# A two-layer diffusion trunk: part of attention's vector work moved to GpSimd, and the order around it

## The chip, the cores and the metric

The kernel runs on one core of a Trainium2 chip. The metric is the device time of one execution in microseconds (us); the kernel before took 3193.55 us (median of three runs, 3193.33 to 3194.81). The engines are TensorE (PE in the profile; PEld is its weight load), VectorE (DVE), ScalarE (ACT), GpSimd (POOL) and SyncE (SP), which issues the DMAs. Each takes its instructions in the order of the program, and waits at an instruction whose operands are not ready.

## The reference

Two layers over 1152 tokens: 128 prompt tokens and 1024 sample tokens, which share the weights. A layer projects the normalised tokens, runs three head groups (latent attention, a short convolution, retention), then an output projection and a SwiGLU mixer, all in float32. The change touches attention alone. For each of 8 heads:

```
q = rmsnorm(rmsnorm(q_lat) @ w_q_up, q_head_g)              # 96 per head: 64 plain + 32 rotary
k, v = ckv @ w_kv_up ; k = rmsnorm(concat(k_nope, k_pe), k_head_g)
sample: q, k rotated on the 32 columns; keys = 1024 sample + 128 cached context tokens
prompt: keys = its own 128 tokens, not rotated
p = softmax(q k^T * 96**-0.5) ; out = p @ v
```

## The kernel before

Heads are worked in four pairs. `pair_prep` (L930) makes q, k and v of a pair: for ten tiles of 128 tokens, nine or three matmuls, copies by ScalarE, and sums of squares (L978, L980). Then come the steps that this text calls the pair's chain: the mean squares (L983 to L986), an inverse square root in 11 small instructions (`rsq`, L231), the rotary steps (`rope`, L911: two products of 128x256 and two sums of 128x128 for each of two halves), and the products of q and k with the inverse norms (L994 to L997). `prompt` (L1008) scales the prompt's own q and k (L1015 to L1018), transposes them on TensorE (L1021) and does the prompt's whole attention in three steps. All these elementwise steps are VectorE's.

`head_prep` (L1056) transposes a head's k and q (L1069), splits them into a high and a low part (L1072 on ScalarE, L1073 on VectorE), and finds the maximum of each query's scores: 24 matmuls (L1080), each followed by a VectorE reduction (L1082); the maxima are negated (L1087), transposed (L1089) and written as eight more rows of q (L1091). `head_main` (L1097) then goes over nine key tiles: six matmuls for the scores (L1126 to L1128), two exponentials on ScalarE (L1129), and, one tile later in `pv`, the product with v (L1109) and the sum of the exponentials of all key tiles into `acc`, eight additions of 128x1024 on GpSimd (L1112, L1118); the last is halved between GpSimd and VectorE (L1116). `head_end` (L1145) multiplies `acc` with ones (L1152), takes the reciprocal by Ln, Exp and one Newton step (L1156 to L1159) and scales the output (L1161). It is issued within the next head, by `finish` after that head's first scores (L1131).

The parts are generators. `attention` (L1167) advances a head's nine tiles step by step (18 steps) and lets the next head's preparation and the next pair's preparation run a set number of steps beside it (`RA`, `RB`); a pair is `ready` `GAP` = 5 steps after its chain, and its prompt part follows. The instructions so issued are then placed by a scheduler that works with estimated durations, so each engine's order can differ from the order of the code. The first pair of a layer is prepared within the input projection (`in_proj`, L811), beside matmuls of L227 to L229 and the convolution (L829 to L838); pairs 2 to 4 within heads 1 to 4 of `attention`. PSUM has three buffers for scores (`mm`) and five for everything else (`ax`); the exponentials, `acc`, the query tiles and raw weights share twelve buffers `W`.

Of the kernel before, what the change touches and what calls it, by code (L numbers as in the profile page):

```python
# [39 lines left out]
EPS = 1e-6  # L40
SCALE = 96.0 ** -0.5
# [35 lines left out]
class Net:  # L77
# [165 lines left out]

# [666 lines left out]

    def rope(self, x, tab, out=None):  # L911

        nc = self.nc
# [3 lines left out]
        nc.vector.tensor_tensor(t1, x, tab[:, 0].unsqueeze(2).to_broadcast(sh), op=ALU.mult)  # L917
        nc.vector.tensor_tensor(t2, x, tab[:, 1].unsqueeze(2).to_broadcast(sh), op=ALU.mult)
        nc.vector.tensor_tensor(out[:, :, :, 0:16], t1[:, :, :, 0:16], t2[:, :, :, 16:32], op=ALU.subtract)
        nc.vector.tensor_tensor(out[:, :, :, 16:32], t2[:, :, :, 0:16], t1[:, :, :, 16:32], op=ALU.add)  # L920

# [8 lines left out]
    def pair_prep(self, l, p, R):  # L930

        nc = self.nc
        wh, wl = self.pair_weights(l, p, R)
        qh, ql = R["qn"]
# [18 lines left out]
        for t in range(10):  # L953
# [28 lines left out]
        V = nc.vector  # L982
        V.tensor_tensor(ssq[:, 2:4, :], ssq[:, 2:4, :], R["kvs2"].unsqueeze(1).to_broadcast([P, 2, 10]), op=ALU.mult)  # L983
        V.tensor_tensor(ssq[:, 2:4, :], ssq[:, 2:4, :], R["kpss"].unsqueeze(1).to_broadcast([P, 2, 10]), op=ALU.add)
        V.tensor_scalar(ssq[:, 2:4, :], ssq[:, 2:4, :], 1.0 / 96, EPS, ALU.mult, ALU.add)
        V.scalar_tensor_tensor(ssq[:, 0:2, 0:9], ssq[:, 0:2, 0:9], 1.0 / 96,  # L986
                               R["qms"].unsqueeze(1).to_broadcast([P, 2, 9]), ALU.mult, ALU.add)
# [20 lines left out]
    def prompt(self, l, p, R):  # L1008
# [3 lines left out]
        at = self.attn_tile(p, R)  # L1012
        gains = self.gains(l)
        for hh in range(2):
            V.tensor_tensor(pr[:, hh, 64:96], pr[:, hh, 64:96], R["gq"], op=ALU.mult)  # L1015
            V.tensor_scalar(pr[:, hh, :], pr[:, hh, :], r[:, hh, 0:1], None, ALU.mult)
            V.tensor_scalar(pr[:, 2 + hh, 0:64], pr[:, 2 + hh, 0:64], r[:, 2 + hh, 0:1], None, ALU.mult)
            V.tensor_scalar(pr[:, 2 + hh, 64:96], R["kper"][:, 0, :], r[:, 2 + hh, 0:1], None, ALU.mult)  # L1018
        pt = self.ax((96, 4, P))
# [36 lines left out]
    def head_prep(self, l, h, R):  # L1056
# [20 lines left out]
        for qt in range(8):  # L1077
# [8 lines left out]
        nc.vector.reduce_max(mn, mx, axis=AX.X)  # L1086
        nc.vector.tensor_scalar(mn, mn, -1.0, None, ALU.mult)  # L1087
# [3 lines left out]
        nc.vector.tensor_tensor(  # L1091
            qh[96:104, :].rearrange("p (a b) -> p a b", b=P), pt.unsqueeze(1).to_broadcast([8, 8, P]),
            self.vec[0:8, o:o + 8].unsqueeze(2).to_broadcast([8, 8, P]), op=ALU.mult)
        R["T", h] = (qh, ql, kh, kl)
        yield CM

    def head_main(self, l, h, R):  # L1097
# [8 lines left out]
        def pv(kt):  # L1106
            for qc in range(2):
                qs = slice(qc * 512, (qc + 1) * 512)
                nc.tensor.matmul(po[64 * qc:64 * qc + 64, :], vv[:, kt, b:b + 64], prs[kt][:, qs],  # L1109
                                 start=(kt == 0), stop=(kt == 8))  # L1110
            if kt == 1:
                nc.gpsimd.tensor_tensor(acc, prs[0], prs[1], op=ALU.add)  # L1112
            elif kt == 8:
                for e, eng in enumerate((nc.gpsimd, nc.vector)):
                    s = slice(512 * e, 512 * e + 512)
                    eng.tensor_tensor(acc[:, s], acc[:, s], prs[kt][:, s], op=ALU.add)  # L1116
            elif kt > 1:
                nc.gpsimd.tensor_tensor(acc, acc, prs[kt], op=ALU.add)  # L1118
        for kt in range(9):
# [3 lines left out]
            for qc in range(2):  # L1123
# [21 lines left out]
    def head_end(self, h, R, po, acc):  # L1145
# [8 lines left out]

        y, t = self.Tt("dy", (P, 512)), self.Tt("dt", (P, 512))
# [11 lines left out]
    def attention(self, l, R, x):  # L1167
# [10 lines left out]
        def pairs():  # L1178
            for p in range(1, 4):
                yield from self.pair_prep(l, p, R)  # L1180
                if p < 3:
                    self.pair_weights(l, p + 1, R)
                for _ in range(GAP):
                    yield
                R["ready", p] = True
                yield
                yield from self.prompt(l, p, R)
            while self.head_lim < 7:
                yield
            yield from self.mix_load(mix, range(6), A)  # L1190
# [570 lines left out]
```

## Time and profile before

| | |
|---|---|
| runs | 3193.33, 3193.55, 3194.81 us |
| the profiled execution | 3189.09 us, span 3187.2 us, mean granted clock 0.975 |
| busy share of the span | PE 96%, PEld 84%, DVE 56%, POOL 37%, ACT 35% |
| the chain that ended last | PE 80%, DVE 13%, ACT 2%, DMA 2%, POOL 1% |
| attention of the two layers | about 368 to 705 us and 1940 to 2280 us |

A stretch's row gives each engine's busy time and the granted TensorE clock as a share of 2.4 GHz (0.5 is the level of 1.2 GHz). Idle time of PE and time at the lower clock are what a stretch can give back; a busy PE is not always at its peak.

### The profile page before, as it was taken

How to read it: one execution, taken by the hardware profiler on the slowest of the kernel's cores; microseconds unless marked ns; L12 is line 12 of the kernel's file. 1: busy time of each engine (PE TensorE's matmuls, PEld its weight loads, DVE VectorE, ACT ScalarE, POOL GpSimd, SP SyncE). 2: the span in 40 equal slices, each digit the busy share in tenths (PEclk: the TensorE clock that was granted, in tenths of full speed). 3: DMA queues.
4: the chain of work that ended last, by engine and by line, in shares of the span. 5: the costliest groups of instructions: out<-in, count | busy, mean ns of one | idle time of the engine just before them, and what ended most of it. 6: DMA issues, size and time to landing. Idle time of an engine off the chain costs nothing.

```text
span 3187.2 us, 48870 instructions
## 1 busy us (share of the span) xinstructions
PE 3045.1 (96%) x19136; PEld 2692.7 (84%) x19136; DVE 1794.0 (56%) x3555; ACT 1112.9 (35%) x2646; POOL 1179.8 (37%) x764
## 2 busy tenths in 40 slices
PE   6999998999799999999999999889998999999999
PEld 5878855459799999998999897554697999999999
DVE  6264466776855455643272655767578554546343
ACT  4323354353432222321153234554344222223211
POOL 3111244455643434311242113435656434343212
PEclk9999998999899999999999999989998999999999
DMA  5323100123221222476231110001322222226323
GB/s 210 115 71 102 54 12 5 53 84 120 71 82 64 82 83 74 171 257 231 74 113 48 31 49 12 12 11 50 108 100 79 83 80 68 66 78 218 99 68 100
DMA packets 126726, 278.07 MB, mean 87 GB/s; under 512 B 24096, under 2 KB 47392, under 8 KB 126496
## 3 DMA queue, kind: packets, MB, share of 16 engines
q1 hardware_dynamic: 126496, 274.95, 25.6%
q8 instruction: 151, 2.47, 0.3%
q14 instruction: 79, 0.65, 0.1%
HBM read 222.57 MB, written 52.33 MB: 86 GB/s over the span
## 4 chain that ended last, share of the span: by engine, by line
PE 80%; DVE 13%; ACT 2%; DMA 2%; issue 2%; POOL 1%; SPq 0%; DVEq 0%; POOLq 0%; ACTq 0%
PE mm L227 14%; PE mm L229 14%; PE mm L228 13%; PE ax L229 6%; PE ax L227 6%; PE ax L228 6%; PE ax L1109 5%; PE ax L1080 2%; PE mm L1126 2%; PE mm L1128 2%; PE mm L1127 2%; PE ax L340 1%; PE ax L1069 1%; DVE mx L1082 1%; POOL W L213 1%
## 5 line engine op out<-in xcount | busy, mean ns | idle before, releaser
L213 POOL TENSOR_TENSOR W<-r,W 128x512 fp32r<-128x512 f32 x336 | 447.4, 1345 | 541.2 <-ACT W L212 530.0
L213 POOL TENSOR_TENSOR W<-W,W 128x640 fp32r<-128x640 f32 (+5 forms) x168 | 299.4, 1783 | 825.7 <-ACT W L212 479.9
L227 PE MATMUL mm<-gh,W 128*128 128x384 f32 x1056 | 354.8, 336 | 2.4 <-DVE u L1400 1.4
L229 PE MATMUL mm<-gh,W 128*128 128x384 f32 x1056 | 353.3, 335 | 0.9 <-POOL W L213 0.8
L228 PE MATMUL mm<-gl,W 128*128 128x384 f32 x1056 | 352.9, 334 | 0.0
L1245 DVE SCALAR_TENSOR_TENSOR x<-mm,mod,x 128x128 f32<-128x128 f32 (+2 forms) x320 | 158.1, 515 | 333.2 <-PE mm L229 331.1
L229 PE MATMUL ax<-hth,W 128*128 128x288 f32 x1056 | 314.2, 298 | 9.5 <-POOL W L213 9.5
L227 PE MATMUL ax<-hth,W 128*128 128x288 f32 x1056 | 315.0, 298 | 7.6 <-ACT W L212 7.6
L228 PE MATMUL ax<-htl,W 128*128 128x288 f32 x1056 | 314.1, 297 | 0.0
L1118 POOL TENSOR_TENSOR W<-W,W 128x1024 f32<-128x1024 f32 x96 | 231.3, 2410 | 222.5 <-ACT W L1129 220.8
L212 ACT CAST W<-W 128x640 fp32r<-128x640 f32 (+5 forms) x168 | 131.5, 784 | 402.4 <-DMA W<-in_w_down 177.9
L212 ACT CAST W<-r 128x512 fp32r<-128x512 f32 x336 | 205.4, 621 | 182.0 <-DMA r<-in_w_up 62.4
L1082 DVE TENSOR_REDUCE mx<-ax 128x1 f32<-128x384 f32 x384 | 195.7, 550 | 115.3 <-PE ax L1080 113.0
L1129 ACT ACTIVATE W<-mm 128x512 f32<-128x512 f32 x288 | 168.5, 606 | 217.8 <-PE mm L1128 210.4
L227 PE MATMUL mm<-hh,W 128*128 128x384 f32 x704 | 243.4, 346 | 0.0
L229 PE MATMUL mm<-hh,W 128*128 128x384 f32 x704 | 242.2, 344 | 0.0
L228 PE MATMUL mm<-hl,W 128*128 128x384 f32 x704 | 241.9, 344 | 0.0
L1109 PE MATMUL ax<-W,vt 128*64 128x512 f32 x576 | 208.6, 658 | 8.3 <-DVE attn L1161 6.7
L229 PEld LDWEIGHTS ax<-hth,W 128*128 128x128 f32 x1056 | 200.8, 190 | 10.7 <-POOL W L213 10.7
L227 PEld LDWEIGHTS mm<-gh,W 128*128 128x128 f32 x1056 | 198.2, 188 | 13.5 <-issue 10.2
L227 PEld LDWEIGHTS ax<-hth,W 128*128 128x128 f32 x1056 | 201.2, 191 | 8.5 <-ACT W L212 8.5
L228 PEld LDWEIGHTS ax<-htl,W 128*128 128x128 f32 x1056 | 201.3, 191 | 0.0
(333 smaller groups left out, 7886.9 us busy)
## 6 DMA issues: line engine op xcount, KB each, us to landing
W<-in_ada_w SPq DMA_DIRECT2D x80, 512.0 KB, 5.1
gr<-gd SPq DMA_DIRECT2D x44, 576.0 KB, 5.5
r<-in_w_gate SPq DMA_DIRECT2D x96, 256.0 KB, 2.8
r<-in_w_up SPq DMA_DIRECT2D x96, 256.0 KB, 4.1
W<-in_w_in_fm SPq DMA_DIRECT2D x30, 512.0 KB, 3.8
W<-in_w_down SPq DMA_DIRECT2D x48, 320.0 KB, 3.8
gd<-gu SPq DMA_DIRECT2D x22, 576.0 KB, 3.7
gd<-gu SPq DMA_DIRECT2D x44, 224.0 KB, 2.2
```

The costliest lines, as they stand in the source:

```text
L212: self.nc.scalar.copy(hi, raw)
L213: self.nc.gpsimd.tensor_tensor(lo, raw, hi.bitcast(F32), op=ALU.subtract)
L227: self.nc.tensor.matmul(ps, wh, xh, start=first and i == 0, stop=False)
L228: self.nc.tensor.matmul(ps, wh, xl, start=False, stop=False)
L229: self.nc.tensor.matmul(ps, wl, xh, start=False, stop=last and i == n - 1)
L1080: nc.tensor.matmul(ps, qh[0:96, qt * P:(qt + 1) * P], kh[0:96, c * CH:(c + 1) * CH], start=True, stop=True)
L1082: nc.vector.reduce_max(mx[:, qt, c:c + 1], ps, axis=AX.X)
L1109: nc.tensor.matmul(po[64 * qc:64 * qc + 64, :], vv[:, kt, b:b + 64], prs[kt][:, qs], start=(kt == 0), stop=(kt == 8))
L1118: nc.gpsimd.tensor_tensor(acc, acc, prs[kt], op=ALU.add)
L1126: nc.tensor.matmul(ps, kh[0:104, ks], qh[0:104, qs], start=True, stop=False)
L1129: nc.scalar.activation(pr[:, qs], ps, AF.Exp, scale=SCALE)
L1245: self.nc.vector.scalar_tensor_tensor(x[m][:, t0:t1], ps[:, t0 - c * CH:t1 - c * CH], self.mod[l][:, j, m, i:i + 1], x[m][:, t0:t1], ALU.m ...
```

## The change

- The pair's chain runs on GpSimd (`G`), and its inverse square root is Ln and Exp on ScalarE with two Newton steps of four GpSimd instructions. `rope` takes the engine as an argument; the tables' own rotary steps, once a layer, stay on VectorE.
- The prompt's scaling of q and k runs on GpSimd, the negation of its maxima and the scaling of its probabilities on ScalarE; the part is cut into more steps, is issued right after the chain, and a pair is `ready` only after it (`GAP` is gone).
- The last addition into `acc` is whole and on GpSimd. `head_end` is issued after the next head's second scores and first product with v. Its Newton step works in place in PSUM (`pd`).
- The maxima are negated in the instruction that spreads them (L1087 goes).

The diff's core (in the rest of it `rope`'s four and `prompt`'s eight instructions change engine):

```
-RA, RB, LEAD, GAP = 1.3, 0.7, 14, 5
+RA, RB, LEAD = 1.3, 0.7, 14
+    def rsq_act(self, ms, shape):
+        G = self.nc.gpsimd
+        y, t = self.sm("rsy", shape), self.sm("rst", shape)
+        self.nc.scalar.activation(t, ms, AF.Ln)
+        self.nc.scalar.activation(y, t, AF.Exp, scale=-0.5)
+        for _ in range(2):
+            G.tensor_tensor(t, y, y, op=ALU.mult)
+            G.tensor_tensor(t, t, ms, op=ALU.mult)
+            G.tensor_scalar(t, t, -0.5, 1.5, ALU.mult, ALU.add)
+            G.tensor_tensor(y, y, t, op=ALU.mult)
...
-        r = self.rsq(ssq, (P, 4, 10))
+        r = self.rsq_act(ssq, (P, 4, 10))
...
-            V.tensor_tensor(q[b], q[b], bc(0, 4, 96), op=ALU.mult)
+            G.tensor_tensor(q[b], q[b], bc(0, 4, 96), op=ALU.mult)
...
+        yield
+        yield
         pt = self.ax((96, 4, P))
...
-            elif kt == 8:
-                for e, eng in enumerate((nc.gpsimd, nc.vector)):
-                    s = slice(512 * e, 512 * e + 512)
-                    eng.tensor_tensor(acc[:, s], acc[:, s], prs[kt][:, s], op=ALU.add)
...
-            if kt == 0:
-                self.finish()
             yield
             if kt:
                 pv(kt - 1)
+                if kt == 1:
+                    self.finish()
                 yield
...
-        nc.vector.tensor_tensor(t, y, pd, op=ALU.mult)
-        nc.vector.scalar_tensor_tensor(y, t, 2.0, y, ALU.subtract, ALU.mult)
+        nc.vector.tensor_tensor(pd, y, pd, op=ALU.mult)
+        nc.vector.scalar_tensor_tensor(y, pd, 2.0, y, ALU.subtract, ALU.mult)
...
-                for _ in range(GAP):
-                    yield
+                yield
+                yield from self.prompt(l, p, R)
                 R["ready", p] = True
                 yield
-                yield from self.prompt(l, p, R)
```

What it does to the engines' orders is shown at three places. On PE, at layer 1's first pair, the transposes of the first head's keys (`kt`, L1069 before, L1086 now) among the projection's matmuls (L227 to L229), before:

```order
L229 MATMUL mm_2804<-hh_462,W_2435 128x384
L1069 MATMUL ax_2834<-ident_76,kt_2467 96x128 x4
L227 MATMUL mm_2864<-hh_232,W_2696 128x384
L228 MATMUL mm_2864<-hl_236,W_2696 128x384
L229 MATMUL mm_2864<-hh_232,W_2697 128x384
L1069 MATMUL ax_2841<-ident_76,kt_2468 96x128 x4
L1069 MATMUL ax_2848<-ident_76,kt_2468 96x128
L227 MATMUL mm_2864<-hh_233,W_2696 128x384
```

and now:

```order
L229 MATMUL mm_2804<-hh_462,W_2435 128x384
L1086 MATMUL ax_2834<-ident_76,kt_2467 96x128 x4
L1086 MATMUL ax_2841<-ident_76,kt_2468 96x128 x4
L1086 MATMUL ax_2848<-ident_76,kt_2468 96x128
L227 MATMUL mm_2864<-hh_232,W_2696 128x384
L228 MATMUL mm_2864<-hl_236,W_2696 128x384
```

The projection's three matmuls that stood between the transposes of the two halves of k now stand behind all nine.

On PE, where head 0 ends and head 1 begins (second pair), before: the last product with v of head 0 (L1109), scores of head 1 (L1126 to L1128), the end of head 0 (L1152):

```order
L1109 MATMUL ax_3377<-W_3798,vt_2469 64x512 x2
L1126 MATMUL mm_3837<-W_3392,kTh_3390 128x512
L1127 MATMUL mm_3837<-W_3393,kTh_3390 128x512
L1128 MATMUL mm_3837<-W_3392,kTl_3391 128x512
L1126 MATMUL mm_3842<-W_3392,kTh_3390 128x512
L1127 MATMUL mm_3842<-W_3393,kTh_3390 128x512
L1128 MATMUL mm_3842<-W_3392,kTl_3391 128x512
L1152 MATMUL ax_3847<-W_3378,ones_78 64x512 x2
L1126 MATMUL mm_3865<-W_3392,kTh_3390 128x512
```

and now (scores L1138 to L1140, v L1125, end of head 0 L1164, the prompt's transposes of the second pair L1037):

```order
L1138 MATMUL mm_3839<-W_3391,kTh_3389 128x512
L1139 MATMUL mm_3839<-W_3392,kTh_3389 128x512
L1140 MATMUL mm_3839<-W_3391,kTl_3390 128x512
L1138 MATMUL mm_3860<-W_3391,kTh_3389 128x512
L1139 MATMUL mm_3860<-W_3392,kTh_3389 128x512
L1140 MATMUL mm_3860<-W_3391,kTl_3390 128x512
L1138 MATMUL mm_3865<-W_3391,kTh_3389 128x512
L1139 MATMUL mm_3865<-W_3392,kTh_3389 128x512
L1140 MATMUL mm_3865<-W_3391,kTl_3390 128x512
L1125 MATMUL ax_3831<-W_3833,vt_2469 64x512 x2
L1164 MATMUL ax_3872<-W_3377,ones_78 64x512 x2
L1037 MATMUL ax_3882<-ident_76,qt_3429 96x128 x4
```

The end of head 0 has moved behind the second key tile's scores and the first product with v of head 1, and the four prompt transposes of the second pair, which stood after three key tiles of head 1 (L1021), follow it at once.

On POOL at the same place, before: head 0's seven whole additions end, then the half one (L1116), and the next weights' low part:

```order
L1118 TENSOR_TENSOR W_3378<-W_3378,W_3758 128x1024
L1116 TENSOR_TENSOR W_3378<-W_3378,W_3798 128x512
L945 MEMSET ssq_4770 128x40
L213 TENSOR_TENSOR qwl_3861<-W_3858,qwh_3860 128x640
L1075 MEMSET kTh_3891 8x1152
L1112 TENSOR_TENSOR W_3835<-W_3836,W_3864 128x1024
```

and now, from head 0's last addition (L1130) on: the inverse root (L251 to L254) and rotary steps (L932, L933) of the second pair:

```order
L1130 TENSOR_TENSOR W_3377<-W_3377,W_3796 128x1024
L251 TENSOR_TENSOR rst_3785<-rsy_3784 128x40
L932 TENSOR_TENSOR qt_3430<-rp_628_3819,rp_629_3820 128x8x16
L252 TENSOR_TENSOR rst_3785<-rst_3785,ssq_3434 128x40
L933 TENSOR_TENSOR qt_3430<-rp_629_3820,rp_628_3819 128x8x16
L253 TENSOR_SCALAR rst_3785<-rst_3785 128x40
L254 TENSOR_TENSOR rsy_3784<-rsy_3784,rst_3785 128x40
L251 TENSOR_TENSOR rst_3785<-rsy_3784 128x40
L252 TENSOR_TENSOR rst_3785<-rst_3785,ssq_3434 128x40
L253 TENSOR_SCALAR rst_3785<-rst_3785 128x40
```

Further behind these, and in front of head 1's first addition, stand the six products of L1007 to L1010 (128x768, 512, 256, 768, 640, 320) and six prompt scalings (L1030 to L1032).

## Rows read from the trace of the kernel before

**Rows 1.** Stretches: span, busy of PE, PEld, DVE, ACT, POOL, clock, DMA.

```profile
360.00:430.00 70.00, 65.92 (x329) 44.30 (x328) 45.51 (x86) 40.09 (x153) 31.16 (x16) 0.95 0.04 14
430.00:540.00 110.00, 99.18 (x437) 58.54 (x436) 78.47 (x143) 54.08 (x200) 43.03 (x21) 0.91 0.03 9
540.00:700.00 160.00, 150.86 (x605) 79.77 (x605) 115.03 (x194) 80.12 (x219) 82.15 (x40) 0.98 0.16 61
...
1865.00:2280.00 415.00, 391.27 (x1795) 253.86 (x1796) 278.75 (x506) 194.36 (x636) 166.52 (x80) 0.95 0.09 33
```

**Rows 2.** PE's waits, 290 to 705 us: total, times, longest.

```profile
PE ax L1080 <- DVE mx L1082: 7.1, 4, 3.2
PE ax L1089 <- DVE kt L997: 3.9, 1, 3.9
PE ax L1069 <- DVE kt L997: 3.7, 2, 2.8
PE ax L1109 <- DVE attn L1161: 3.4, 1, 3.4
```

**Rows 3.** One line's instructions on VectorE, L1159: durations in ns min/median/max.

```profile
L1159 DVE SCALAR_TENSOR_TENSOR dy<-dt,dy x16: 679/1588/2803, 422.4 to 2286.4; 128x512 f32<-128x512 f32 x16
```

**Rows 4.** POOL in order of time, second pair: start, us, instruction, idle before.

```profile
405.08 2.39 POOL L1118 TENSOR_TENSOR W<-W,W 128x1024 f32<-128x1024 f32 x1 [2.15 <-ACT W L1129]
407.54 1.43 POOL L1116 TENSOR_TENSOR W<-W,W 128x512 f32<-128x512 f32 x1
...
416.96 2.90 POOL L1112 TENSOR_TENSOR W<-W,W 128x1024 f32<-128x1024 f32 x1
```

**Rows 5.** VectorE in order of time, the last of the second pair's chain.

```profile
417.58 2.62 DVE L997 TENSOR_TENSOR kt<-kper,rsy 128x320 f32<-128x320 f32 x1
```

**Rows 6.** POOL groups by shape: busy, mean ns, idle before.

```profile
L213 POOL TENSOR_TENSOR W<-W,W 128x1024 fp32r<-128x1024 f32 x50 | 121.0, 2422 | 369.0 <-ACT W L212 187.6 <-PE mm L228 69.5 <-PE mm L229 47.5
...
L213 POOL TENSOR_TENSOR W<-W,W 128x384 fp32r<-128x384 f32 x32 | 33.0, 1032 | 64.1 <-ACT W L212 64.1
...
L213 POOL TENSOR_TENSOR W<-W,W 128x512 fp32r<-128x512 f32 x16 | 20.6, 1289 | 75.1 <-ACT W L212 75.1
```

**Rows 7.** VectorE groups by shape, 290 to 430 us.

```profile
L1082 DVE TENSOR_REDUCE mx<-ax 128x1 f32<-128x384 f32 x48 | 24.0, 551 | 22.0 <-PE ax L1080 21.9
...
L994 DVE TENSOR_TENSOR qt<-qt,rsy 128x768 f32<-128x768 f32 x4 | 3.8, 953 | 0.1
...
L837 DVE SCALAR_TENSOR_TENSOR yc<-gc,vec,yc 128x1023 f32<-128x1023 f32 x2 | 2.6, 1276 | 0.0
...
L918 DVE TENSOR_TENSOR rp<-qt,rtabq 128x256 f32<-128x256 f32 x4 | 1.7, 418 | 0.0
...
L996 DVE TENSOR_TENSOR kt<-kt,rsy 128x512 f32<-128x512 f32 x2 | 1.4, 684 | 0.0
...
L919 DVE TENSOR_TENSOR qt<-rp,rp 128x128 f32<-128x128 f32 x4 | 1.1, 284 | 0.0
```

**Rows 8.** PE in order of time at the second pair.

```profile
406.52 1.94 PE L1109 MATMUL ax<-W,vt 128*64 128x512 f32 x8
408.38 0.50 PE L1126 MATMUL mm<-W,kTh 104*128 104x512 f32 x1
...
409.66 0.39 PE L1128 MATMUL mm<-W,kTl 96*128 96x512 f32 x1
409.98 1.75 PE L1152 MATMUL ax<-W,ones 128*64 128x512 f32 x4
...
420.35 1.06 PE L1069 MATMUL ax<-ident,kt 128*96 128x128 f32 x4 [2.83 <-DVE kt L997]
422.63 0.42 PE L1021 MATMUL ax<-ident,qt 128*96 128x128 f32 x1 [1.22 <-DVE qt L1016]
```

**Rows 9.** VectorE in order of time, where the first pair's chain starts.

```profile
297.34 0.18 DVE L983 TENSOR_TENSOR ssq<-ssq,kvs 128x20 f32<-128x20 f32 x1
```

**Rows 10.** PE in order of time at the first pair: transposes of the keys.

```profile
303.66 0.61 PE L1069 MATMUL ax<-ident,kt 128*96 128x128 f32 x4
...
305.67 0.51 PE L1069 MATMUL ax<-ident,kt 128*96 128x128 f32 x3 [0.87 <-DVE kt L997]
```

More of the change, by code (lines that the diff above doesn't have):

```diff
@@ L241, in rsq @@
             V.scalar_tensor_tensor(y, t, 1.5, y, ALU.add, ALU.mult)
+        return y
+    def rsq_act(self, ms, shape):
[8 more added lines that the diff above has]
+            G.tensor_tensor(y, y, t, op=ALU.mult)
         return y
@@ L909, in mla_tables, with rope @@
         R["rtab"], R["gq"] = tabq, gq
-    def rope(self, x, tab, out=None):
-        nc = self.nc
+    def rope(self, x, tab, out=None, eng=None):
+        V = eng or self.nc.vector
         out = x if out is None else out
@@ L916, in rope @@
         t1, t2 = self.Tt("rp1", sh), self.Tt("rp2", sh)
[L917 to L920, printed above, removed]
+        V.tensor_tensor(t1, x, tab[:, 0].unsqueeze(2).to_broadcast(sh), op=ALU.mult)
+        V.tensor_tensor(t2, x, tab[:, 1].unsqueeze(2).to_broadcast(sh), op=ALU.mult)
+        V.tensor_tensor(out[:, :, :, 0:16], t1[:, :, :, 0:16], t2[:, :, :, 16:32], op=ALU.subtract)
+        V.tensor_tensor(out[:, :, :, 16:32], t2[:, :, :, 0:16], t1[:, :, :, 16:32], op=ALU.add)
     def pair_weights(self, l, p, R):
@@ L981, in pair_prep @@
             yield
[L982 to L987, printed above, removed]
-        r = self.rsq(ssq, (P, 4, 10))
+        G = nc.gpsimd
+        G.tensor_tensor(ssq[:, 2:4, :], ssq[:, 2:4, :], R["kvs2"].unsqueeze(1).to_broadcast([P, 2, 10]), op=ALU.mult)
+        G.tensor_tensor(ssq[:, 2:4, :], ssq[:, 2:4, :], R["kpss"].unsqueeze(1).to_broadcast([P, 2, 10]), op=ALU.add)
+        G.tensor_scalar(ssq[:, 2:4, :], ssq[:, 2:4, :], 1.0 / 96, EPS, ALU.mult, ALU.add)
+        G.tensor_scalar(ssq[:, 0:2, 0:9], ssq[:, 0:2, 0:9], 1.0 / 96, None, ALU.mult)
+        G.tensor_tensor(ssq[:, 0:2, 0:9], ssq[:, 0:2, 0:9], R["qms"].unsqueeze(1).to_broadcast([P, 2, 9]), op=ALU.add)
+        r = self.rsq_act(ssq, (P, 4, 10))
         yield
         for b in range(2):
-            self.rope(q[b][:, :, :, 64:96], R["rtab"][:, :, 4 * b:4 * b + 4])
+            self.rope(q[b][:, :, :, 64:96], R["rtab"][:, :, 4 * b:4 * b + 4], eng=G)
             t0, n = 1 + 4 * b, 4 + b
             bc = lambda i, n, m: r[:, i:i + 2, t0:t0 + n].rearrange("p a b -> p b a").unsqueeze(3).to_broadcast([P, n, 2, m])
-            V.tensor_tensor(q[b], q[b], bc(0, 4, 96), op=ALU.mult)
+            G.tensor_tensor(q[b], q[b], bc(0, 4, 96), op=ALU.mult)
             yield
-            V.tensor_tensor(k[b][:, :, :, 0:64], k[b][:, :, :, 0:64], bc(2, n, 64), op=ALU.mult)
-            V.tensor_tensor(k[b][:, :, :, 64:96],
+            G.tensor_tensor(k[b][:, :, :, 0:64], k[b][:, :, :, 0:64], bc(2, n, 64), op=ALU.mult)
+            G.tensor_tensor(k[b][:, :, :, 64:96],
                             R["kper"][:, t0:t0 + n, :].unsqueeze(2).to_broadcast([P, n, 2, 32]), bc(2, n, 32), op=ALU.mult)
@@ L1013, in prompt @@
         gains = self.gains(l)
+        G = nc.gpsimd
         for hh in range(2):
[L1015 to L1018, printed above, removed]
+            G.tensor_tensor(pr[:, hh, 64:96], pr[:, hh, 64:96], R["gq"], op=ALU.mult)
+            G.tensor_scalar(pr[:, hh, :], pr[:, hh, :], r[:, hh, 0:1], None, ALU.mult)
+            G.tensor_scalar(pr[:, 2 + hh, 0:64], pr[:, 2 + hh, 0:64], r[:, 2 + hh, 0:1], None, ALU.mult)
+            G.tensor_scalar(pr[:, 2 + hh, 64:96], R["kper"][:, 0, :], r[:, 2 + hh, 0:1], None, ALU.mult)
+        yield
+        yield
         pt = self.ax((96, 4, P))
@@ L1030, in prompt @@
         V.reduce_max(m, ps, axis=AX.X)
-        V.tensor_scalar(m, m, -SCALE, None, ALU.mult)
+        nc.scalar.mul(m, m, -SCALE)
         pp = self.Tt("pp", (P, 2, P))
@@ L1037, in prompt @@
         for hh in range(2):
-            V.tensor_scalar(pp[:, hh, :], pp[:, hh, :], den[:, hh:hh + 1], None, ALU.mult)
+            nc.scalar.activation(pp[:, hh, :], pp[:, hh, :], AF.Copy, scale=den[:, hh:hh + 1])
+        yield
         yield
@@ L1090, in head_prep @@
         o, _ = VEC["eye8"]
-        nc.vector.tensor_tensor(
-            qh[96:104, :].rearrange("p (a b) -> p a b", b=P), pt.unsqueeze(1).to_broadcast([8, 8, P]),
-            self.vec[0:8, o:o + 8].unsqueeze(2).to_broadcast([8, 8, P]), op=ALU.mult)
+        nc.vector.scalar_tensor_tensor(
+            qh[96:104, :].rearrange("p (a b) -> p a b", b=P), pt.unsqueeze(1).to_broadcast([8, 8, P]), -1.0,
+            self.vec[0:8, o:o + 8].unsqueeze(2).to_broadcast([8, 8, P]), ALU.mult, ALU.mult)
         R["T", h] = (qh, ql, kh, kl)
@@ L1153, in head_end @@
                              start=True, stop=True)
-        y, t = self.Tt("dy", (P, 512)), self.Tt("dt", (P, 512))
+        y = self.Tt("dy", (P, 512))
         nc.scalar.activation(y, pd, AF.Ln)
         nc.scalar.activation(y, y, AF.Exp, scale=-1.0)
-        nc.vector.tensor_tensor(t, y, pd, op=ALU.mult)
-        nc.vector.scalar_tensor_tensor(y, t, 2.0, y, ALU.subtract, ALU.mult)
+        nc.vector.tensor_tensor(pd, y, pd, op=ALU.mult)
+        nc.vector.scalar_tensor_tensor(y, pd, 2.0, y, ALU.subtract, ALU.mult)
         for qc in range(2):
@@ L1182, in pairs @@
                     self.pair_weights(l, p + 1, R)
-                for _ in range(GAP):
-                    yield
+                yield
+                yield from self.prompt(l, p, R)
                 R["ready", p] = True
                 yield
-                yield from self.prompt(l, p, R)
             while self.head_lim < 7:
```

1 line of the change is left out of this document (removed).

## Prediction

> **What bounds the kernel now.** I read first the page's busy shares: PE is busy for 96% of the span, so only its waits and the time at its lower clock can be given back. Next the table of stretches [rows 1], which puts both into attention: PE idles 70.0 − 65.9 = 4.1 us in 360 to 430, 10.8 in 430 to 540, 9.1 in 540 to 700. The granted clock there is 0.95, 0.91 and 0.98; with two levels (1.2 and 2.4 GHz) the loss is about (1 − clock) × span = 3.5, 9.9 and 3.2 us. That is 24.0 + 16.6 = 40.6 us, with the first pair's 0.9 [rows 10] 41.5 us a layer. Layer 2 has the same shape (23.7 us idle and 0.95 in its stretch) [rows 1].
>
> Then PE's waits [rows 2]: the reader is to see that VectorE ends nearly every one (score maxima, the chain's last products, the scaled output). Then VectorE's durations: L1159, always 512 elements, takes from 0.68 to 2.80 us [rows 3]. At 417.58 the chain's last product, 320 elements, takes 2.62 us [rows 5] and lies under a GpSimd addition that itself took 2.90 in place of 2.39 [rows 4]. VectorE's 768 elements took 0.95 elsewhere [rows 7]. So the two engines slow each other, and VectorE is late in part because GpSimd adds.
>
> **The price of the chain on GpSimd.** No row shows a rotary step or a product with a broadcast operand on GpSimd. The nearest are its plain two-operand instructions: 384 elements 1.03 us, 512 1.29, 1024 2.42 [rows 6], so 2.21 ns an element ((2.42 − 1.29) / 512) and about 0.16 us fixed. From this line, a pair: mean squares five of about 0.2, 1.0; inverse root eight of 0.25, 2.0; rotary four of 256 (0.72) and four of 128 (0.44), 4.6; q two of 768 (1.85), 3.7; k 512, 640, 256 and 320 (1.29, 1.57, 0.72, 0.86), 4.4; prompt scalings eight small ones, 1.8. Sum 17.6 us.
>
> On VectorE undisturbed [rows 7]: rotary 4 × 0.42 + 4 × 0.28 = 2.8; q 1.9; k about 2.4 (0.68 for 512, the rest along the line through 768); fifteen small ones at 0.18 [rows 9], 2.7; prompt about 1.2. Sum 11.0. This is the lower bound of the chain on GpSimd. For the upper I take its products 1.5 times dearer: 17.6 + 0.5 × 12.7 = 24. I take 17.6, since all rows of GpSimd itself lie on that line.
>
> **First pair.** The chain starts at 297.3 on VectorE [rows 9], its query part some 0.7 us earlier, and nothing else is long on GpSimd there. The first half of k is ready after mean squares, root, both rotaries, one q and two k products: about 11.2 us from 296.6, at 307.8; the second half 1.85 + 1.57 + 0.86 later, at 312.1. PE comes to these transposes at 303.66, and in the old order waited 0.87 once, before the second half [rows 10]. Now both stand together, with the projection's three matmuls behind them: PE waits 4.1, transposes, and waits 3.9 more. 8.0 against 0.9 is +7.1, and an idle this long has its price in the clock: by 430 to 540, where 10.8 idle stands beside 9.9 of clock loss, up to as much again; by 540 to 700, a third of it. I take 2, near the latter, since all waits there too are short: **+9 us**.
>
> **Second pair.** GpSimd begins its seventh addition at 405.08 [rows 4]. In its new order follow then: that addition (2.39, to 407.5), the mean squares but one and half the rotary steps (4.4, to 411.8), head 0's last addition, whole now (2.39 in place of 1.43 [rows 4], to 414.2), the rest of root and rotary (3.0), the six products (8.1), the prompt scalings (1.8): 427.2. PE does head 1's first scores from 408.38 to 410.0 [rows 8], the second's to 411.4 and one product with v to 412.2. Head 0's end waits until 414.2 (2 us), and takes 1. The pair's prompt transposes follow at 415.2 and wait until 427.2, 12 us. Before, these two were 2.83 and 1.22 [rows 8]. 13.9 against 4.05 is **+10 us**; I leave the clock as it was. What waits behind the transposes on PE is head 1's main loop, ready long since: the wait is not filled. GpSimd's additions for head 1 come late too, which costs buffers W, not PE, as long as three or four are free.
>
> **The later pairs and heads (430 to 700).** Here the change gives. VectorE loses the chains, the half additions and the prompt's scalings; what stays mostly reads PSUM, the maxima at a steady 0.55 us [rows 7]. Before: 10.8 + 9.1 idle and 9.9 + 3.2 clock, 33 us. After, for pair 3: prompt transposes wait about 2.4 us and the following head's end 3.5 (a backlog of 17.6 and three additions of 2.4 against the time of a head); for pair 4 a head's end about 3.9; clock loss beside these about 5; what does not hang on the pairs (the mixer's loads, the last head) stays near 8. Sum 23: **−10 us**. The maxima's negation (eight small VectorE instructions) and the Newton step in place of PSUM lie here and are in this sum; by themselves they are at most 8 × 0.18 = 1.4 and the stretch of L1159 (median 1.59 against 0.68, eight heads, 7 us a layer, of which PE waits 3.4 [rows 2]). ScalarE takes over twelve small instructions a pair; it is busy 54 of 110 us [rows 1], and I cost them at nothing; uncovered it would be 2 us a layer.
>
> **Sum.** +9 + 10 − 10 = +9 us a layer, +18 for two. On the profiled execution, 3189.1, that is 3207; the runs' median lies 4.5 above it, so **3211.5 us**. With the chain at 11.0 us the three terms become about +1, −1 and −15, so −31 in all: 3163. At 24 us each pair waits 6.4 more, where all of it shows: +26 a layer on top, so 3212 + 52 = 3264, the upper bound. The break-even lies near 15 us a pair.
>
> **A rule beside the rows.** L1159's 2.80 us and L997's 2.62 beside a 2.90 us addition [rows 3 to 5] show each engine holding up the other. The Trainium skill, SBUF — State Buffer, "SBUF: two separate sides", says that VectorE and GpSimd share a pair of ports under an exclusive lock, where whichever comes first keeps the other out for its whole instruction; by it VectorE instructions that read PSUM alone go free. The trace agrees as far as it goes: the maxima, which read PSUM, stay at 0.55. The rule speaks for the change in the main loop, and against it in the first pair, where the convolution's VectorE instructions remain; that is rival 4.
>
> **The rivals.**
> 1. Faster: relief of VectorE decides. If GpSimd does the chain in under about 15 us a pair, prompt transposes come when ready and the 41.5 us shrink. For it: PE's waits are on VectorE throughout [rows 2], and VectorE's instructions stretch up to fourfold [rows 3]. Against it: every GpSimd row is about twice VectorE's price [rows 6, 7]. 3163 us.
> 2. No net change: the main loop gives back 19 where I put 10, by fewer waits on maxima (7.1) and on the output (3.4) [rows 2]; 3194 us. Against it: those two are only 10.5 of the 33, and the end of a head now hangs on one more GpSimd half addition.
> 3. Dearer GpSimd: broadcast operands cost 1.5 times, the backlog reaches the buffers W, and the exponentials wait too: about three quarters of the way to that bound, 3250 us. For it: GpSimd goes from 43 of 110 us [rows 1] to about 43 + 2 × 17.6 and the larger last additions, some 80 of 110. Against: no row shows such a price.
> 4. The first pair's chain held by the convolution: L837 and its like, 1.28 us each [rows 7], stand in VectorE among these steps; two to four of them held in full add 1.3 to 2.6 us to each wait at PE, about +3 a layer: 3217 us.
>
> **Chances.** My forecast (3200 to 3225) 0.35, rival 4 0.08, rival 3 0.12, rival 1 0.33, rival 2 0.12. The forecast's own range is 3197 to 3230, if the chain's price is off by 2 us either way. 0.2% of the time, 6.4 us, is about what a measurement of this kernel tells from no change: faster by more 0.33, within 0.12, slower by more 0.35 + 0.08 + 0.12 = 0.55. To leave no more than 2 in 10 out, the range goes from 3165, most of the way to rival 1, to 3245, most of the way to rival 3.
>
> **What would show it.** At the first pair PE's row at the keys' transposes should name GpSimd's products with two waits near 4 us; at the second, the prompt's transposes should wait near 12 us for a GpSimd scaling, and head 0's end near 2 for the last addition. The waits of L1080 on VectorE's maxima should nearly go, and L1159's successor stay near 0.7 us. GpSimd's products of 768 should take 1.85 us: at 1.2 or less the first rival holds, at 2.8 the third. The prediction is wrong if the prompt transposes wait under 4 us at the second pair, or if 430 to 700 gives back more than 18 us a layer.

## The result and the profile after

The changed kernel took 3210.82 us (median of five runs, 3208.02 to 3212.28) against 3193.55 (median of five, 3191.41 to 3200.70). The ratio estimated from all these runs is 1.0052, 95% interval 1.0041 to 1.0062, so 13 to 20 us slower. In a later set of runs of both it was 1.0037 (1.0023 to 1.0051). The forecast was 3211.5. The total came out. Of its three terms the first held, the second had the size but not the whole cause, and the third was about half of what the experiments showed, which a blockage that nobody foresaw hid in one of the two layers.

The stretches of [rows 1] in the changed kernel, with the first pair's put in front (columns as there):

```profile
290.00:330.00 40.00, 33.74 (x186) 30.89 (x185) 12.83 (x22) 9.59 (x38) 21.42 (x36) 0.87 0.21 67
360.00:430.00 70.00, 59.50 (x321) 43.42 (x319) 23.42 (x43) 35.71 (x149) 36.91 (x43) 0.95 0.04 14
430.00:540.00 110.00, 106.73 (x479) 62.71 (x478) 52.59 (x96) 62.72 (x236) 68.65 (x66) 0.97 0.03 9
540.00:700.00 160.00, 141.43 (x563) 75.81 (x562) 90.01 (x149) 74.27 (x191) 95.15 (x71) 0.95 0.16 58
```

VectorE is relieved as meant: 23.4 us in place of 45.5, 52.6 in place of 78.5. PE's idle time has not gone with it; it has moved, out of 430 to 540 (10.8 to 3.3 us) into 360 to 430 (4.1 to 10.5) and 540 to 700 (9.1 to 18.6). PE's waits over the same stretch as [rows 2] (what waits, for whom, total, times, longest):

```profile
PE ax L1097 <- DVE mx L1099: 13.5, 2, 11.6
PE ax L1037 <- POOL qt L1030: 9.9, 2, 9.1
PE ax L1086 <- POOL kt L1010: 6.3, 2, 4.0
PE ax L1105 <- DVE mn L1103: 4.3, 2, 3.8
```

The waits of the score matmuls for a maximum have not gone: they are 13.5 us for 7.1, 11.6 of it at once, and 1.9 beside that. Two waits are new, both for GpSimd: the prompt's transposes and the first pair's transposes. The Newton step, which took 0.68 to 2.80 us [rows 3], now lies in PSUM and is steady (its duration in ns, min/median/max):

```profile
L1171 DVE SCALAR_TENSOR_TENSOR dy<-ax,dy x16: 675/686/692, 433.8 to 2300.8; 128x512 f32<-128x512 f32 x16
```

PE at the first pair, in order of time, for [rows 10]:

```profile
304.63 1.09 PE L1086 MATMUL ax<-ident,kt 128*96 128x128 f32 x4 [3.98 <-POOL kt L1010]
308.00 1.30 PE L1086 MATMUL ax<-ident,kt 128*96 128x128 f32 x5 [2.28 <-POOL kt L1010]
308.96 0.67 PE L227 MATMUL mm<-hh,W 128*128 128x384 f32 x1
```

These are two waits, 6.26 us in all, for the forecast's 8.0. A transpose group that took 0.61 us takes 1.09 behind the first of them. The granted clock from 305 to 310 us is at the lower level, 0.50:

```profile
305.00:310.00 5.00, 2.72 (x12) 2.24 (x11) 0.90 (x2) 1.55 (x4) 5.00 (x8) 0.50 0.00 0
```

PE at the second pair, for [rows 8]:

```profile
417.35 1.08 PE L1125 MATMUL ax<-W,vt 128*64 128x512 f32 x4
419.38 1.08 PE L1164 MATMUL ax<-W,ones 128*64 128x512 f32 x4 [0.95 <-POOL W L1130]
429.56 0.45 PE L1037 MATMUL ax<-ident,qt 128*96 128x128 f32 x1 [9.10 <-POOL qt L1030]
430.81 1.20 PE L1037 MATMUL ax<-ident,qt 128*96 128x128 f32 x3 [0.80 <-POOL qt L1030]
```

The prompt's transposes wait 9.9 us (12 forecast), the end of head 0 waits 0.95 (2 forecast). GpSimd's chain of the first pair, its first row and the products:

```profile
292.91 0.27 POOL L999 TENSOR_SCALAR ssq<-ssq 128x18 f32<-128x18 f32 x1 [0.36 <-ACT sqj L991]
...
301.50 1.48 POOL L1007 TENSOR_TENSOR qt<-qt,rsy 128x768 f32<-128x768 f32 x1
302.94 1.06 POOL L1009 TENSOR_TENSOR kt<-kt,rsy 128x512 f32<-128x512 f32 x1
303.95 0.63 POOL L1010 TENSOR_TENSOR kt<-kper,rsy 128x256 f32<-128x256 f32 x1
...
307.93 0.52 POOL L1030 TENSOR_SCALAR qt<-qt,rsy 128x96 f32<-128x96 f32 x1
```

From 292.91 to 307.93 is 15.0 us, and with the six scalings from there to 310.46 the chain takes 17.6 us: the forecast's sum, with cheaper products (1.48 for 1.85) and dearer scalings (2.5 for 1.8).

To give each stage its time, the table takes the starts of fixed matmuls, the same in every kernel. "To head 0" runs from one matmul of the projection (L227, at 275.7 us in before) to head 0's first scores, "head 1" from its first scores to head 2's, and so on (the third matmul of a score tile, L1128 before and L1140 now); the last stage ends with head 7's last scores. Each cell is layer 1 / layer 2 in us, from one profile. A profile is a single execution, so stages are compared by this table and whole kernels by the medians of their runs. The kernels below the first four rows are those of the experiments.

| kernel | to head 0 | head 1 | heads 2, 3 | head 4 | heads 5 to 7 | the rest of the span |
|---|---|---|---|---|---|---|
| before | 93.2 / 67.1 | 52.1 / 52.2 | 102.6 / 102.4 | 38.2 / 38.2 | 100.8 / 103.1 | 2357.3 |
| before, again | 93.1 / 67.1 | 52.2 / 52.1 | 96.9 / 102.3 | 39.3 / 38.2 | 102.4 / 103.1 | 2361.2 |
| changed | 100.9 / 73.9 | 64.8 / 65.6 | 87.8 / 87.9 | 51.1 / 44.5 | 95.3 / 91.8 | 2363.2 |
| changed, again | 100.4 / 74.0 | 64.7 / 65.7 | 87.9 / 87.9 | 51.0 / 44.5 | 95.3 / 91.8 | 2364.2 |
| first pair on VectorE | 92.8 / 66.5 | 64.4 / 64.5 | 87.9 / 87.8 | 50.9 / 43.2 | 95.3 / 91.8 | 2363.5 |
| all pairs on VectorE | 92.3 / 66.4 | 60.9 / 60.0 | 101.3 / 102.7 | 38.5 / 37.3 | 91.8 / 96.7 | 2365.3 |
| key product on GpSimd | 99.9 / 73.3 | 64.3 / 65.3 | 87.9 / 87.8 | 41.6 / 42.8 | 91.7 / 92.0 | 2355.6 |
| old place of the prompt | 100.0 / 73.6 | 47.5 / 47.0 | 99.0 / 98.8 | 43.2 / 39.3 | 98.5 / 100.3 | 2360.4 |
| before, prompt early | 93.2 / 67.1 | 60.8 / 60.7 | 106.4 / 106.4 | 36.7 / 36.7 | 97.0 / 97.0 | 2362.1 |
| before, head's end | 92.8 / 67.0 | 56.6 / 57.3 | 99.0 / 100.2 | 36.6 / 36.6 | 100.5 / 98.9 | 2364.4 |
| mixed | 92.5 / 66.5 | 45.5 / 46.2 | 99.1 / 99.2 | 40.1 / 40.1 | 94.5 / 94.1 | 2363.0 |
| mixed, two steps | 92.5 / 66.5 | 54.0 / 55.0 | 95.7 / 96.3 | 37.9 / 37.9 | 91.8 / 96.6 | 2365.3 |
| mixed, third pair late (three) | 92.5 / 66.5 | 45.9 / 45.7 | 94.6 / 94.6 | 44.8 / 44.7 | 99.8 / 99.8 | 2363.6 |
| mixed, third pair late (five) | 92.4 / 66.5 | 45.8 / 46.1 | 97.9 / 98.1 | 48.7 / 48.8 | 97.5 / 97.5 | 2367.1 |

The rest of the span holds none of these stages and wanders from 2356 to 2367 us over these fourteen profiles, and by 4 us between the two of before; it is left out of what follows. Head 0's stage is left out: 40.1 us in before, 40.7 in the changed kernel. The attention columns repeat within 0.6 us in the changed kernel and in layer 2 of before; in layer 1 of before they differ by 1.1 us in head 4, 1.6 in heads 5 to 7 and 5.7 in heads 2 and 3.

### The profile page after: what moved, and what is told of

It is laid out like the page before. It is cut to its first block, busy times and chain, and to the rows that moved or that the text cites. A ratio compares the mean times of both kernels' runs of the same rounds, so it can differ in the third digit from the quotient of the medians.

```text
span 3208.1 us, 48843 instructions
## 1 busy us (share of the span) xinstructions
PE 3048.5 (95%) x19136; PEld 2701.3 (84%) x19136; DVE 1625.5 (51%) x3203; ACT 1122.1 (35%) x2686; POOL 1325.3 (41%) x1044
## 4 chain that ended last, share of the span: by engine, by line
PE 74%; DVE 8%; POOL 4%; issue 2%; ACT 2%; DMA 1%; SPq 0%; POOLq 0%; DVEq 0%; ACTq 0%
PE mm L227 12%; PE mm L228 12%; PE mm L229 12%; PE ax L227 6%; PE ax L229 6%; PE ax L228 6%; PE ax L1125 5%; PE ax L1097 2%; PE mm L1138 2%; PE mm L1139 2%; PE mm L1140 2%; PE ax L1086 1%; POOL W L213 1%; PE ax L353 1%; DVE mh L1240 1%
## 5 line engine op out<-in xcount | busy, mean ns | idle before, releaser
L213 POOL TENSOR_TENSOR W<-r,W 128x512 fp32r<-128x512 f32 x336 | 448.1, 1347 | 545.9 <-ACT W L212 529.0
L213 POOL TENSOR_TENSOR W<-W,W 128x640 fp32r<-128x640 f32 (+5 forms) x168 | 299.5, 1784 | 815.3 <-ACT W L212 484.4
L227 PE MATMUL mm<-gh,W 128*128 128x384 f32 x1056 | 356.1, 337 | 3.6 <-DVE u L1411 2.4
L229 PE MATMUL mm<-gh,W 128*128 128x384 f32 x1056 | 354.7, 336 | 0.9 <-POOL W L213 0.8
L1130 POOL TENSOR_TENSOR W<-W,W 128x1024 f32<-128x1024 f32 x112 | 266.9, 2383 | 174.6 <-ACT W L1141 164.7
L229 PE MATMUL ax<-hth,W 128*128 128x288 f32 x1056 | 315.6, 299 | 10.3 <-POOL W L213 10.3
L227 PE MATMUL ax<-hth,W 128*128 128x288 f32 x1056 | 315.6, 299 | 7.3 <-ACT W L212 7.3
L227 PE MATMUL mm<-hh,W 128*128 128x384 f32 x704 | 244.3, 347 | 0.0
L229 PE MATMUL mm<-hh,W 128*128 128x384 f32 x704 | 242.7, 345 | 0.0
L1125 PE MATMUL ax<-W,vt 128*64 128x512 f32 x576 | 215.1, 631 | 0.0
L229 PEld LDWEIGHTS ax<-hth,W 128*128 128x128 f32 x1056 | 202.1, 192 | 11.4 <-POOL W L213 11.4
L227 PEld LDWEIGHTS mm<-gh,W 128*128 128x128 f32 x1056 | 199.2, 189 | 14.7 <-issue 12.0
L227 PEld LDWEIGHTS ax<-hth,W 128*128 128x128 f32 x1056 | 202.0, 191 | 8.2 <-ACT W L212 8.2
```

Of the source, the lines that this page charges most:

```text
L213: self.nc.gpsimd.tensor_tensor(lo, raw, hi.bitcast(F32), op=ALU.subtract)
L227: self.nc.tensor.matmul(ps, wh, xh, start=first and i == 0, stop=False)
L229: self.nc.tensor.matmul(ps, wl, xh, start=False, stop=last and i == n - 1)
```

## Experiments

Each expectation sets a theory A against a rival B; the text behind it says which of them came true.

**The key product on GpSimd.** The 11.6 us wait in layer 1's head 4, VectorE in order of time:

```profile
566.24 1.49 DVE L1099 TENSOR_REDUCE mx<-ax 128x1 f32<-128x384 f32 x3
578.85 2.32 DVE L918 TENSOR_TENSOR kper<-kpe,vec 128x32 f32<-128x32 f32 x1 [11.13 <-POOL qt L1032]
581.09 2.40 DVE L1099 TENSOR_REDUCE mx<-ax 128x1 f32<-128x384 f32 x5
```

This L918 belongs to layer 2. Its tile `kper` has one buffer, which layer 1's last prompt scaling on GpSimd still reads; VectorE stands at it, and the maxima and PE behind it. The experiment moves this one instruction to GpSimd:

```
-            nc.vector.tensor_tensor(kr[:, i, :], kpe[:, i, :], gk, op=ALU.mult)
+            (nc.gpsimd if i else nc.vector).tensor_tensor(kr[:, i, :], kpe[:, i, :], gk, op=ALU.mult)
```

> The changed kernel with one instruction moved: the product of the cached context's rotary key with its gain (128x32, line L918, the copy for the tenth tile) on GpSimd instead of VectorE. In the changed kernel that instruction for layer 2 stands in VectorE's order in the middle of layer 1's head 4, waits 11.1 us there for GpSimd's last prompt scaling, and PE waits 11.64 us for the maxima behind it. Theory A (an instruction that nobody needs yet blocks VectorE's queue): that wait goes, with some clock, so 8 to 12 us less than the changed kernel, 3199 to 3203 us; layer 2 unchanged. Rival B (PE would have waited there anyway, for the last addition or the scaled output, as in layer 2's 3.0 us): 0 to 4 us less, 3207 to 3211 us, with another wait of 8 us or more at the same place.

It took 3198.03 us, 1.0014 of before (0.9998 to 1.0029), which is just under A's 3199. Layer 1's head 4 went from 51.1 to 41.6 and heads 5 to 7 from 95.3 to 91.7, so A came true. B holds for a part: PE then waits 3.0 us for the last addition, as in layer 2.

**The old place of the prompt part**, all chains still on GpSimd.

```
-                yield
+                for _ in range(5):
+                    yield
+                R["ready", p] = True
+                yield
                 yield from self.prompt(l, p, R)
-                R["ready", p] = True
-                yield
```

> The changed kernel with the old place of the prompt part: five steps after the pair's chain the pair is ready, and the prompt follows. On PE the second pair's prompt transposes then stand some 28 rows of matmuls later. Theory A (PE waits at those transposes only because they stand too early): the 9.9 us at the second pair's transposes fall under 4 in each layer and with the clock the kernel gets 10 to 16 us faster than the changed one, 3195 to 3201 us. Rival B (the chain's length itself is what PE waits for): the wait moves to the next thing that needs it, the third head's transposes, or the other pairs get worse; 3207 to 3214 us.

It took 3191.59 us, 0.9995 (0.9985 to 1.0006): faster than A's range. Head 1's stage fell by 17.3 and 18.6 us, to 5 below before, with the chain still on GpSimd. B came true later: heads 2 and 3 grew by 11, where GpSimd's next chain stands before a head's last addition:

```profile
517.45 1.98 PE L1164 MATMUL ax<-W,ones 128*64 128x512 f32 x4 [9.26 <-POOL W L1130]
```

**The first pair on VectorE**; `self.rsq` in place of `rsq_act` for it too, and the same choice in the prompt's scalings.

```
-        G = nc.gpsimd
+        G = nc.vector if p == 0 else nc.gpsimd
```

> The changed kernel with the first pair's chain, inverse root and prompt scaling (of each layer) on VectorE, as before the change; the other pairs stay on GpSimd. Theory A (the first pair's longer chain costs PE its 6.3 us of waiting and the clock behind it): 5 to 8 us a layer less, 3195 to 3201 us, and the granted clock of 290 to 330 us back at 1.00 from 0.87. Rival B (the time at the first pair is made up later, because the stretch behind it is limited by something else): 0 to 3 us less.

It took 3191.43 us, 1.0001 (0.9991 to 1.0012). The stage to head 0 fell by 8.1 and 7.4 us, and the stretch's clock is back at 1.00:

```profile
290.00:330.00 40.00, 38.76 (x232) 36.14 (x232) 23.15 (x61) 11.68 (x38) 4.91 (x3) 1.00 0.27 94
```

A came true, with a little more than its range: the other stages gave 3 us beside. All of them together fell by 18.5 us, the median by 19.4 (15.4 against the second set of the changed kernel).

**All pairs on VectorE** (as above, for every pair).

> The changed kernel with all four pairs' chains, inverse roots and prompt scalings on VectorE; the end of a head, the last addition on GpSimd, the prompt's smaller steps and its earlier place stay as changed. Theory A (the chain's place is what costs): back to the kernel before or a little better, 3183 to 3196 us. Rival B (the later end of a head with its whole last addition on GpSimd, or the prompt's early place, costs): 3203 us or more.

It took 3189.02 us, 0.999 (0.998 to 0.9999): A by the time. But head 1's stage stayed at 60.9 us, 8.8 above before, with this wait on PE and these products on VectorE:

```profile
422.89 0.42 PE L1037 MATMUL ax<-ident,qt 128*96 128x128 f32 x1 [8.35 <-DVE qt L1030]
```

```profile
413.06 2.27 DVE L1007 TENSOR_TENSOR qt<-qt,rsy 128x768 f32<-128x768 f32 x1
415.25 2.82 DVE L1009 TENSOR_TENSOR kt<-kt,rsy 128x512 f32<-128x512 f32 x1
418.00 2.56 DVE L1010 TENSOR_TENSOR kt<-kper,rsy 128x256 f32<-128x256 f32 x1
420.48 0.95 DVE L1007 TENSOR_TENSOR qt<-qt,rsy 128x768 f32<-128x768 f32 x1
```

The same 768 elements take 2.27 us and 0.95. Beside GpSimd's work (additions of 3.05 and 2.67 us lie in the same 7 us) VectorE's chain is not the 11.0 us of the forecast but some 5.5 more: the first three products took 7.65, for about 2.1. From the table's start of head 1 to the transposes it is 14.3 us here (408.58 to 422.89) and 15.3 with GpSimd's chain (414.22 to 429.56), so up to there the engine makes 1 us; over the whole stage it makes 3.9 and 5.6. And heads 2 and 3 take 101 to 103 us with VectorE's chains, 88 with GpSimd's: that is the relief of VectorE, since the engine of the chains and the kind of their roots are all that differs.

**Before, with the prompt part early**: only the last `if` of the change.

```
-                for _ in range(GAP):
-                    yield
-                R["ready", p] = True
                 yield
                 yield from self.prompt(l, p, R)
+                R["ready", p] = True
+                yield
```

> The kernel before with one thing of the change: the prompt part issued right behind the pair's chain, the pair ready only after it; all chains on VectorE. Theory A (the early place of the prompt part itself makes PE wait, whatever engine does the chain: 8.35 us at the second pair's prompt transposes also with the chain on VectorE): the stage of head 1 (52.1 us before) grows by 5 to 10 us in each layer, PE's wait at the second pair's prompt transposes is 5 us or more; time 3196 to 3212 us. Rival B (the loss at the second pair comes from the chain's length on GpSimd): the wait stays under 3 us, the time within 4 us of before.

It took 3205.98 us, 1.0039 (1.0026 to 1.0052): A came true. On the kernel before, this edit alone costs about 13 us. Head 1's stage grew by 8.7 and 8.5, and its wait is the one seen twice already, now for VectorE:

```profile
425.43 0.42 PE L1021 MATMUL ax<-ident,qt 128*96 128x128 f32 x1 [8.69 <-DVE qt L1016]
```

**Before, with the head's end alone**: the end issued in `kt == 1`, the last addition whole on GpSimd, `pd` in place, the maxima negated where they are spread (as in the change).

> The kernel before with the head's end alone changed: issued after the second key tile's scores, the last addition whole on GpSimd, the Newton step in place in PSUM, the maxima negated where they are spread. Theory A (this part gives back VectorE's time: scaled outputs and maxima come sooner): PE's waits on the scaled output (3.4 us) and part of those on maxima (7.1 us) go, 4 to 8 us a layer, 3178 to 3187 us. Rival B (a half addition more on GpSimd and the later end only move the wait): within 4 us of before, with PE waiting for the last addition.

It took 3191.55 us, 0.9994 (0.9983 to 1.0006): A's gain is not there. The Newton step is steady here too (673 to 691 ns), and PE's wait on the scaled output is gone, but PE's waits for VectorE's last products of k rose from 6.7 us (L997 in [rows 2], less the 0.9 of [rows 10]) to 9.0, from 374 to 712 us:

```profile
PE ax L1069 <- DVE kt L997: 9.0, 3, 3.1
```

So B for the time; but PE did not wait for the last addition. Head 1's stage alone grew by 4.5 and 5.1 us, where PE's waits for k at head 2's transposes went from 2.8 to 6.1 us; in layer 2, where the profiles of before agree, the later stages gave 8.0 back for these 5.1.

**Mixed**: the changed kernel with the first pair on VectorE, the key product on GpSimd, and the old place of the prompt part for the second pair only (`if p == 1:` before the five steps).

> The changed kernel with three edits: the first pair's chain and prompt scalings on VectorE, the tenth tile's rotary key product on GpSimd, and for the second pair alone the old place of the prompt part (five steps after the chain, the pair ready first); third and fourth pair as changed. By the stages of the profiles so far, against the changed kernel: to head 0 6.8 us less, head 1's stage 17 less, head 4's and 7's in layer 1 9.6 and 3 less, so 60 us less over both layers if nothing comes back: 3151 us. Theory A (the three losses are separate): 3150 to 3165 us, faster than the kernel before by 0.9% or more. Rival B (they are one backlog that moves on, as the 9.3 us at a head's end that the old place of all prompt parts brought): 3175 us or more.

It took 3162.67 us, 0.9899 (0.988 to 0.9918): 30 us faster than before, 48 than the change (44 by its second set), and the fastest of all. A came true, in the upper half of its range: the wait at the second pair became 5.4 us, now at head 2's key transposes, and this one appeared at the third pair's prompt transposes:

```profile
501.13 0.45 PE L1037 MATMUL ax<-ident,qt 128*96 128x128 f32 x1 [9.25 <-POOL qt L1030]
```

**Mixed, two steps** (2 for 5).

> As the mixed kernel, with two steps in place of five between the second pair's chain and its prompt part. Theory A (the transposes must only stand behind what PE can do meanwhile; three steps fewer keep the third pair's chain earlier): within 5 us of the mixed kernel, its head 2 and 3 stages the shorter. Rival B (each step counts): 8 us or more slower, with a wait of 5 us or more at the second pair's prompt transposes.

It took 3171.42 us, 0.9925 (0.991 to 0.9939): B by the time. Head 1 takes 54.0 for 45.5; the wait is at head 2's key transposes (5.24 us) rather than at the second pair's prompt transposes. The third pair's wait fell from 9.3 to 5.1 us, less than head 1 lost.

**Before and the changed kernel again.**

> The kernel before once more, unchanged, for a second profile. The stage behind attention to the end took 908.8 us in the first one and 912.7 to 915.3 in every other kernel, whose work there is the same. Theory A (the first profile was a short execution there, so the 6.5 us that the changed kernel's profile is longer in this stage are no effect of the change): 911 us or more now, and the stages of attention within 0.5 us of the first profile. Rival B (the change costs something there): 908 to 910 us again.

It took 3189.89 us (one run); the part behind attention took 911.95 us, as A has it, and 912.16 in the changed kernel's second profile, so no effect of the change shows there. Layer 1's heads 2 and 3 were 5.7 us shorter, against A's 0.5.

> The changed kernel once more beside these. Theory A: 3206 to 3213 us; attention's stages as in its first profile within 0.5 us each; the stretch between the two attentions, 1249 us in the first, nearer 1242 to 1246 as in the others with the same first pair. Rival B (its first time was a slow session): 3200 us or less.

It took 3206.85 us, 1.0037 (1.0023 to 1.0051), with attention as in the table: A there. The stretch between the attentions was 1248.7 us again, not the 1242 to 1246 of A. Against before's 1239.9 and 1243.0 some 7 us of it are layer 2's first pair; why it is longer than in the two other kernels with the same first pair (1241.9 with the key product on GpSimd, 1245.7 with the old place of the prompt) stays open.

**Mixed, with the third pair late too** (three steps, and five).

> The mixed kernel with the third pair also ready first and its prompt part three steps later. Theory A (the 9.3 us at the third pair's prompt transposes are again an early place): that wait falls under 3 us and the kernel is 8 to 20 us faster than the mixed one, 3143 to 3155 us. Rival B (the backlog on GpSimd moves it to a head's end, as with the old place for all): 3160 us or more with a wait of 6 us or more at the sum of the exponentials.

> The mixed kernel with the third pair also ready first and its prompt part five steps later. Theory A: as with three steps, within 5 us, 3143 to 3158 us. Rival B: five steps push the fourth pair's chain in front of a head's last addition, and PE waits 6 us or more there: 3160 us or more.

These took 3173.43 us, 0.9939 (0.9918 to 0.996), and 3185.57, 0.997 (0.9954 to 0.9985). Both times A fails. The wait at the third pair's prompt transposes went, and one at the fourth pair's came, 6.7 and 9.6 us, of the kind that the delay was to cure; so B's time, at another place. With three steps heads 2 and 3 are 4.5 us shorter than in the mixed kernel, head 4 is 4.7 longer and heads 5 to 7 are 5.3 longer (layer 1). This fits a delay that pushes back what is issued after it; no run isolates that. With five steps:

```profile
595.04 0.45 PE L1037 MATMUL ax<-ident,qt 128*96 128x128 f32 x1 [9.59 <-POOL qt L1030]
```

## Why the prediction was right, and where it was not

**The first pair, +9 us a layer: right.** It was +7.3 to 7.7 in layer 1 and +6.8 to 6.9 in layer 2 (table); with the chain back on VectorE the loss is gone. The first wait was 3.98 us for 4.1. The second was 2.28 for 3.9: GpSimd's three products between the two halves of k took 3.4 us for 4.3, and the transposes between the waits 1.09 us for the 0.4 that the forecast's sum leaves. Beside 5.4 us more of waiting than before (6.26 less 0.87) about 2 are left in layer 1 for the clock, as set down.

**The second pair, +10: near in size, incomplete in cause.** It was +12.6 to 12.7 in layer 1 and +13.4 to 13.6 in layer 2. The forecast made it a matter of the chain's length alone ("With the chain at 11.0 us" this term becomes −1). The runs show that the place of the prompt part decides whether the length is felt. At the new place VectorE's chain gave +8.8 and +7.8 against before, and the new place alone, on the kernel before, +8.7 and +8.5: about two thirds of the loss comes with either engine. At the old place GpSimd's chain of 17.6 us gave −4.6 and −5.2. The parts do not simply add, since the head's end by itself made this stage 4.5 and 5.1 us longer at the old place. No run has a chain of 11.0 us; taking the 5.5 us by which VectorE's chain was stretched off its wait of 8.35 us would leave about 2.9, an estimate. The working had noted that nothing fills this wait, and had not asked what it would be with the old chain.

**The later pairs and heads, −10: the term that was wrong.** Layer 1 gave −7.4 (the table's last three stages, −14.8, +12.9 and −5.5; −4.4 by the second profiles), layer 2 −19.5 (−14.5, +6.3 and −11.3). The relief of VectorE was undersized by about half: heads 2 and 3 alone gave 14.5 in layer 2, whose stages repeat. Layer 1 came near the forecast because L918 stood in VectorE's queue, which the forecast did not see: with that one instruction moved, layer 1's three stages are 20.4 us under before (17.4 under its second profile). The forecast had looked at what GpSimd and PE newly wait for, and not at old VectorE instructions with a new engine to wait for. By the prediction's own sign, more than 18 us given back from 430 to 700, it was wrong in layer 2.

**Sum.** By the table's first profiles +7.7 + 12.7 − 7.4 = +13.0 in layer 1 and +6.8 + 13.4 − 19.5 = +0.7 in layer 2: 13.7 us, and 15 with head 0 (18 by the second profiles). The forecast had 9 in each. That the total is right is partly luck: the missed blockage and the undersized relief lie on opposite sides.

**The working.** Two of its sums are loose, and neither moves the total: its items up to the first half of k add to 11.5 us where it writes 11.2, and the 4.4 us before head 0's last addition are six of the eight rotary steps, not half of them.

**The rivals.** Rival 1, that a short chain gives 3163 us, was not tested: no run has a chain of 11 us on GpSimd. What the runs show is that 11.0 us are a price without neighbours: back on VectorE the chain took some 16.5 us at the second pair, and the kernel 3189. [rows 5] had shown the neighbour. The mixed kernel came to 3162.67 with the later pairs' chains as long as ever. Rival 2 had the main loop right in layer 2 (19, and 19.5 came), though not the time. Rival 3 is refuted by the row of 768 elements at 1.48 us. Rival 4 did not arise: from 290 to 306 us VectorE had three short instructions that read PSUM (0.55 us each), and the convolution's long ones stand behind the chain.

**The two engines at one row.** L918 (its durations in ns, min/median/max) and the GpSimd addition beside its longest case:

```profile
L918 DVE TENSOR_TENSOR kper<-kpe,vec x4: 179/182/2316, 15.4 to 1702.7; 128x32 f32<-128x32 f32 x4
578.78 2.33 POOL L1128 TENSOR_TENSOR W<-W,W 128x1024 f32<-128x1024 f32 x1
```

L918's 32 elements took 2.32 us from 578.85, where its other three cases took 0.18; GpSimd's addition (2.33 us) had begun at 578.78. The maxima, which read PSUM, stayed between 542 and 559 ns all along. The Trainium skill, SBUF — State Buffer, "SBUF: two separate sides", has a VectorE instruction with two SBUF inputs and a GpSimd instruction that reads SBUF lock each other out on shared ports for a whole instruction. The trace agrees to 0.1 us at this row.

## What to carry to other kernels

Price a step that leaves an engine by what it takes there now, beside its neighbours, and not by its undisturbed duration. Where an engine takes its instructions in order, first ask where the consumer of a slower chain stands. Here five steps later for one pair, with two small edits beside (the first pair back on VectorE, the key product moved), turned a loss of 17 us into a gain of 30; a delay for the next pair too gave 11 to 23 us of it back. After moving a reader to another engine, look for every later writer of its tile: one that nobody needs yet can hold a whole queue.

## What was not expected of the hardware

GpSimd's products with the inverse norms, which have a broadcast operand, were faster than its plain two-operand instructions of the same size: 640 elements took 1.27 us, where L213's 640, which write another type (fp32r), took 1.54, and 512 took 1.06, where the addition of 512 before (L1116) took 1.43. The broadcast alone does not explain it: the rotary products, with a broadcast table, took 0.73 for 256 elements, as the plain line has it. The cause stays open. GpSimd's scalings by a column of scalars were dear for their size: 96 elements took 0.52 us, where a rotary sum of 128 took 0.46.
